# Running the first MLP pair in seven products inside the output projection's last units, and dealing out the query norms and gate logarithms

## The chip, the core and the metric

The kernel runs on one core of one Trainium2 chip. The metric is the device time of one execution in microseconds (us). Before the change the median of three runs is 2124.6 us (2124.42 to 2124.96).

Engines are named as in the profile: PE is TensorE's matmul, PEld its weight load, DVE is VectorE, ACT is ScalarE, POOL is GpSimd, and SP is the engine whose queue issues nearly all DMAs here.

## The reference: two layers of a hybrid encoder

256 rows of 2048 numbers go through two layers. All of it is float32:

```python
for l in range(N_A):                       # layer A
    u = rms_norm(h, a_norm_g[l])
    proj = u @ a_w_in[l]
    q, k, v, fz = jnp.split(proj, [D, 2 * D, 3 * D], axis=-1)
    q = rms_norm(q.reshape(B, S, H, Dh), a_q_g[l])
    k = rms_norm(k.reshape(B, S, H, Dh), a_k_g[l])
    logf = jax.nn.log_sigmoid(fz + a_b_f[l])
    o = forgetting_attention(q, k, v, logf)
    h = h + o.reshape(B, S, D) @ a_w_out[l]
    h = h + sq_relu_mlp(h, mlp_norm_g[layer], mlp_w1[layer], mlp_w2[layer])
kv = rms_norm(h, kv_norm_g) @ kv_w          # shared keys and values
...
for l in range(N_B):                       # layer B: own queries, chunked attention
    u = rms_norm(h, b_norm_g[l])
    q = rms_norm((u @ b_w_q[l]).reshape(B, S, H, Dh), b_q_g[l])
    o = chunked_relbias_attention(q, k_sh, v_sh, b_rel[l])
    h = h + o.reshape(B, S, D) @ b_w_out[l]
    h = h + sq_relu_mlp(h, mlp_norm_g[layer], mlp_w1[layer], mlp_w2[layer])
```

`sq_relu_mlp` is `relu(rms_norm(h) @ w1)**2 @ w2` with 8192 hidden columns. The two MLPs are most of the matmul work.

## The kernel before

**Units and panels.** All weights come in *units*: 128 partitions by 1024 numbers, 512 KB, which are two 128-row slices of the contraction by 512 output columns. A float32 unit is split in two parts that TensorE multiplies fast: `hi` (ACT, line 183) and `lo = raw - hi` (DVE, line 184). The activations are split the same way, and each product is three matmuls, hi·hi, hi·lo and lo·hi (`three`, lines 388 to 390). A *panel* is 512 output columns for all 256 rows: eight units, each with 12 matmuls of 128x512 (2 slices, 2 row blocks, 3 matmuls). A panel accumulates in a pair of PSUM banks.

**Order.** The kernel writes the order of PE, DVE, ACT and SP by hand, and each engine runs its list in that order. One iteration of the program handles one unit: `fetch` issues `hi` and `lo` of the unit two places ahead and keeps three raw loads under way, then come the matmuls of this unit, and then `run_fill` runs one entry of the list `fill`. In `fill` stand the small jobs of norms, attention, residuals and transposes, so one entry runs in each unit. There are three `hi` and `lo` buffers: a `hi` waits until PE is done with the unit three places before. When a panel is complete, its two banks are evacuated (`evac`).

**Seven products.** In the MLPs two panels form a *pair* (halves `a` and `b`). The first two units of each half (four units, a 2x2 block scheme in rows and columns) can be computed with seven products in place of eight, by sums of weights and of activations. Each of the seven is a *form* of 6 matmuls. Their weights are 11, T3, T2, T1, 21, T4 and 22, run in this order as f0 to f6. The four raw blocks 11, 12, 21 and 22 are loaded by `bring` (line 739), some 9 to 6 plain units before f0. The sums T1 = 12 − 11, T3 = 22 − 12, T2 = T3 + 11 and T4 = 21 − T2 are made by `make` on DVE (line 754). The forms T3, T2, T1 and 22 multiply by sums of activations: `S` for the layer's normalized input, `Sh` for hidden values (`sums`, line 229: four DVE sums, two ACT copies as the hi part, and one unit later two DVE subtractions as the lo part, line 246). Forms f0 to f3 are woven between the last units (b5, b6, b7) of the pair before; f4 to f6 between the pair's own units. In the kernel before, the first pair of each MLP is not `fast`: it runs all 16 units plainly (a0 a1 b0 b1 …) and leaves only b6 and b7 for weaving. An MLP has 16 pairs: four chunks of hidden columns, in each two pairs of w1 and two of w2.

**The way into the MLP.** The output projection (`stage`, line 424) has four panels: 0 and 1 woven unit by unit, then 2, then 3. After each, `next_x` (line 301) adds the residual, sums squares, transposes the 512 columns (`blocks32` on DVE, then `carry`: `rows` writes to DRAM, `columns` reads back in four DMAs), and two units run `split_turned` (line 249): ACT scales into `bias` (line 254), ACT rounds to hi (line 257), DVE makes lo (line 258). Panel 0 also makes `S`. Panel n gives the activations of contraction units 2n and 2n + 1. `st1.inverse` makes the row scale that the second half of the MLP needs.

**Queries of layer B.** `head_norm` (line 430) squares a panel (ACT), sums per head (DVE, line 444), takes the power on POOL (line 449), multiplies and transposes (DVE, lines 453 and 277). For query panel 0 it first copies the PSUM banks (`qc`, line 437), because panel 2 takes the same banks at once.

**Gate logarithms.** `gates` (line 603) hands `logs` to `fill` in three steps: sums of the products (lines 628 to 634), then Exp, Ln and the scan (636 to 639), then the write to DRAM (642 to 645).

**Buffers that matter.** Pool `qkv` holds two each of tags `k` and `v` (attention; the raw blocks of a pair), `bias` (attention, `split_turned`, T1 and T3). Pool `prob` has one room `p`: attention's, then `Sh`. PSUM has pairs `acc0`, `acc1`, the two banks `s` of attention's logits, and `po`. A pair takes `acc0` and alternately `acc1` or `s`.

Of the kernel before, what the change touches and what calls it, by code (L numbers as in the profile page):

```python
# [15 lines left out]
P = 128  # L16
# [30 lines left out]
def trunk(ctx: ExitStack, tc: tile.TileContext, xT, xr, gs, hg, bf, wgate, w_in, w_oa, w1a, w2a,  # L47
# [53 lines left out]
    def queue(src, first, woven):  # L101
        u = [src[i] for i in range(first, first + KT // UA * NG)]
        n = KT // UA
        if woven:
            u[: 2 * n] = [u[i + q * n] for i in range(n) for q in range(2)]
        units.extend(u)
# [5 lines left out]

    class Pair:

        def __init__(self, src, first, fast, late, third):
            self.src = [[src[first + q * 8 + u] for u in range(8)] for q in range(2)]
            self.fast, self.late, self.third, self.ps, self.t = fast, late, third, None, {}

        def own(self):
            if not self.fast:  # L120
                head, rest = "a0 a1 b0 b1 a2 a3 b2 b3 a4 a5 b4 b5 a6 a7", "b6 b7"
            elif self.late:
                head, rest = "a2 f4 a3 f5 b2 f6 b3 a4 a5 b4 a6 a7", "b5 b6 b7"
            else:
                head, rest = "a2 f4 a3 f5 a4 f6 a5 a6 a7 b2 b3 b4", "b5 b6 b7"
            return [[(self, "abf".index(i[0]), int(i[1])) for i in t.split()] for t in (head, rest)]

    def plan_mlp(w1, w2):
        n, pairs = w1.shape[0] // NCH, []
        for c in range(NCH):  # L130
            for src, late in ((w1, False), (w2, True)):
                for q in range(2):
                    pairs.append(Pair(src, c * n + 16 * q, bool(pairs), late and q == 0, len(pairs) % 2 == 1))
        plan, rest = [], []
        for p in pairs:
            head, mine = p.own()
            if p.fast:
                f = [(p, 2, i) for i in range(4)]
                if len(rest) == 3:
                    plan += [f[0], rest[0], f[1], rest[1], f[2], rest[2], f[3]]  # L140
                else:
                    plan += [f[0], f[1], rest[0], f[2], rest[1], f[3]]
            plan += head
            rest = mine
# [6 lines left out]
    queue(w_oa, 0, True)  # L151
    plan_a = plan_mlp(w1a, w2a)
    queue(w_qb, 0, True)
    for i in range(w_kv.shape[0]):
        units.append(w_kv[i])
    queue(w_ob, 0, True)
    plan_b = plan_mlp(w1b, w2b)
# [143 lines left out]
    def next_x(n, r2, stats, which, into, kept=None, fs=None):  # L301
        add_h = residual(n, r2)
        zt = []
        fs = fs if n == 0 else None

        def use(flipped=False, which=which, into=into):
            t = zt[1].rearrange("p (i k b c) -> p k b i c", i=4, k=GH, b=NB)
            if flipped:
                t = t[:, :, :, ::-1, ::-1]
            return split_turned(t, n, which, into, fs)  # L310

        def turn():
            zt.extend(turned("s" if kept is not None and n >= 2 else "q"))
            for b in range(NB):
                blocks32(h[b][:, n * 512 : (n + 1) * 512], zt[0], b)

        def f(b, ps):
            add_h(b, ps)
            if b == NB - 1:
                step = steps(use)  # L320
                add_fill([[lambda b=b: stats.add(b, n) for b in range(NB)], [turn],
                          [lambda: add_fill(carry(*zt) + [[]] * (3 if n == 1 else 1) + [[step]] * 2 + ([] if fs is None else [[], [], [step], [step]]))]])
                if kept is not None:
                    kept.append(use)
        return f
# [85 lines left out]
    def panels(x, evacs, before=None):  # L411
        ps = [acc_pair() for _ in evacs]
        for u in range(KT // UA):
# [10 lines left out]
    def stage(x, evacs, woven):  # L424
        if woven:
            panels(x, evacs[:2])
        for e in evacs[2 if woven else 0 :]:
            panels(x, [e])

    def head_norm(stats, z, dst, late=0, copied=False, gap=0):  # L430
        rest = []

        def f(b, ps):
            src = ps
            if copied:
                src = wk.tile([P, 512], F32, name="qc", tag="wk")
                V.tensor_copy(src, ps)
            sq = wk.tile([P, 512], F32, name="sq", tag="wk")
            S.activation(sq, src, AF.Square)
            ss = sm.tile([P, GH], F32, name="ss")  # L440
            rn = sm.tile([P, GH], F32, name="rn")

            def total():
                V.tensor_reduce(ss, sq.rearrange("p (a d) -> p a d", a=GH), axis=AX.X, op=ALU.add)

            def norm():
                vv = sm.tile([P, GH], F32, name="vv")
                V.tensor_scalar(vv, ss, 1.0 / P, stats().e[:, b : b + 1], op0=ALU.mult, op1=ALU.add)  # L448
                G.tensor_tensor(rn, vv, mhalf, op=ALU.pow)  # L449

            def turn():
                qn = wk.tile([P, 512], F32, name="qn", tag="wk")
                V.tensor_tensor(qn.rearrange("p (a d) -> p a d", a=GH), src.rearrange("p (a d) -> p a d", a=GH),
                                rn.unsqueeze(2).to_broadcast([P, GH, P]), op=ALU.mult)
                blocks32(qn, z, b)

            rest.append((total, norm, turn))
            if b == NB - 1:
                for total, norm, _ in rest:
                    total()  # L460
                    if not late:
                        norm()
                add_fill([[]] * (late - 1) + ([[n for _, n, _ in rest]] if late else []) + [[]] * gap + [[t] for _, _, t in rest] + carry(z, dst))
        return f
# [138 lines left out]
    def gates(x, st):  # L603
# [21 lines left out]
        def logs():  # L625
# [11 lines left out]
            S.activation(z, z, AF.Ln, bias=1.0)  # L637
            V.scalar_tensor_tensor(z, u, 0.0, z, op0=ALU.min, op1=ALU.subtract)
# [9 lines left out]
        def turn_c():  # L648
            pc = ps_o.tile([P, 512], F32, name="pt", tag="po")
            ct["cq"] = const.tile([P, NB, H], F32, name="cq")  # L650
            for b in range(NB):
# [5 lines left out]
                [], [step], [step], [step], [], [turn_c]]  # L657
# [33 lines left out]

    def mlp(plan, x, Sx, st, last):
        hids = [[] for _ in range(NCH)]
# [33 lines left out]
        pairs = list(dict.fromkeys(p for p, _, _ in plan))  # L727

        def open_pair(p):
# [3 lines left out]
            p.ps = [acc_pair(0), acc_pair(2 if p.third else 1)]  # L733
# [5 lines left out]
        def bring(p, name):  # L739
            t = qkv.tile([P, UN], F32, name="w" + name, tag="kv"[name[1] == "2"], bufs=2)  # L740
            SY.dma_start(t, p.src[int(name[1]) - 1][int(name[0]) - 1])
            p.t[name] = t

        def make(p, name):
            t = p.t
            if name in ("T1", "T3"):
                t[name] = qkv.tile([P, GH * REL], F32, name="w" + name, tag="bias", bufs=2)[:, :UN]
            elif name == "T2":
                t[name] = t["12"]
            else:  # L750
                t[name] = t["11"]
            a, b, op = {"T1": ("12", "11", ALU.subtract), "T3": ("22", "12", ALU.subtract),
                        "T2": ("T3", "11", ALU.add), "T4": ("21", "T2", ALU.subtract)}[name]
            V.tensor_tensor(t[name], t[a], t[b], op=op)  # L754

        ahead = {9: (bring, "12"), 8: (bring, "11"), 7: (bring, "22"), 6: (bring, "21"), 5: (make, "T1"), 2: (make, "T3")}
        starts = [i for i, it in enumerate(plan) if it[1:] == (2, 0)]
        for i, (p, q, u) in enumerate(plan):
# [9 lines left out]
            else:  # L768
# [8 lines left out]
                if nxt is not None:  # L777
                    d = sum(1 for it in plan[i:nxt] if it[1] < 2)
                    if d in ahead:
                        do, name = ahead[d]  # L780
                        do(plan[nxt][0], name)
# [10 lines left out]
    stage(o, [next_x(n, None, st1, 1, x1, fs=S1) for n in range(NG)], True)  # L792
    add_fill([[], [], [], [st1.inverse]])
# [10 lines left out]
    for g in range(NG):  # L804
        box = {}

        def f(b, ps, box=box, g=g):
            if b == 0:
                z, lq = turned("z")
                box["lq"], box["f"] = lq, head_norm(lambda: st2, z, lq, copied=g == 0, gap=2 * (g == 1))  # L810
            box["f"](b, ps)
            if b == NB - 1:
                add_fill([[]] * (7 + 2 * (g == 1)) + [[lambda: qs.append(scale_q(box["lq"], 1, g))]])
        evs.append(f)
    stage(xb, evs, True)
# [23 lines left out]
    stage(o, [next_x(n, None, st3, 4, x3, fs=S3) for n in range(NG)], True)  # L839
    add_fill([[], [], [], [st3.inverse]])  # L840
# [66 lines left out]
```

## Time and profile before

| | |
|---|---|
| median of three runs | 2124.6 us |
| the profiled execution, its own time | 2125.99 us |
| its span | 2124.2 us |
| granted TensorE clock | 1.00 |
| DVE busy | 1574.4 us (74%) |
| ACT busy | 1185.6 us (56%) |
| moved by DMA | 491.61 MB, mean 231 GB/s |

How to read the rows below. A group's row has the line, engine, operation, names written and read, count, then busy us, mean ns of one, and idle time before it with the releaser. A row of the timeline has the start and length in us, the engine, line and names, and in brackets the idle time before it and what ended it. A row of a stretch has its bounds and length, then busy time and count of PE, PEld, DVE, ACT and POOL, the clock, the DMA share and GB/s. Starts are counted from the start of the span.

The order of the work in time: layer A's projections and attention to about 340 us, its output projection to 387, MLP A to about 1108, queries, keys, values and attention of layer B to about 1390, its output projection to 1439, MLP B to the end.

### The profile page before, as it was taken

Reading aid. Unit: us, or ns where it says so; the run is one execution under the profiler, and the core shown is the slowest. Engines: PE = TensorE matmul, PEld = TensorE weight load, DVE = VectorE, ACT = ScalarE, POOL = GpSimd, SP = SyncE. Lnnn points to the kernel's source line nnn. Section 1 sums busy time; section 2 is a strip of 40 time slices with the busy share of each in tenths; the row PEclk is TensorE's granted clock in tenths of the full one; section 3 lists DMA queues with packets and bytes.
Section 4 is the critical chain, followed back from the end, with each engine's and each line's share of the span. In section 5 each row is a group of like instructions: output and inputs, shape, how many; then the busy total and the mean of one; then the engine's idle time right before and its main releaser. Section 6 shows DMA issues by size and latency. Waiting matters only on the chain.

```text
span 2124.2 us, 25852 instructions
## 1 busy us (share of the span) xinstructions
PE 2109.3 (99%) x9338; PEld 1740.9 (82%) x9338; DVE 1574.4 (74%) x1795; ACT 1185.6 (56%) x1421; POOL 48.2 (2%) x47
## 2 busy tenths in 40 slices
PE   9999999999999999999999999999999999999999
PEld 7788888878888888888888888887788888888887
DVE  6677666688787777778767577766877887877775
ACT  6544455565466465556575444455654654664663
POOL 1011000000000000000001000000000000000000
PEclk9999999999999999999999999999999999999999
DMA  8787777876676577577678777777766666766764
GB/s 281 230 256 230 239 246 237 268 229 225 203 247 225 201 246 240 186 236 269 190 227 268 236 234 234 233 244 246 248 224 211 239 225 207 249 220 200 247 239 147
DMA packets 183889, 491.61 MB, mean 231 GB/s; under 512 B 36929, under 2 KB 73937, under 8 KB 183761
## 3 DMA queue, kind: packets, MB, share of 16 engines
q1 hardware_dynamic: 183760, 489.96, 70.7%
q8 instruction: 73, 1.20, 0.2%
q14 instruction: 56, 0.45, 0.1%
HBM read 450.01 MB, written 39.87 MB: 231 GB/s over the span
## 4 chain that ended last, share of the span: by engine, by line
PE 93%; DVE 3%; DMA 1%; ACT 1%; issue 1%; SPq 0%; ACTq 0%; DVEq 0%
PE acc L390 25%; PE acc L389 25%; PE acc L388 25%; PE s L389 6%; PE s L390 6%; PE s L388 6%; DVE lo L184 1%; DMA raw<-in_w_in 1%; ACT hi L183 1%; PE po L532 1%; PE s L501 1%; PE po L533 0%; PE s L500 0%; DVE wT L754 0%; DVE z L277 0%
## 5 line engine op out<-in xcount | busy, mean ns | idle before, releaser
L184 DVE TENSOR_TENSOR lo<-raw,hi 128x1024 fp32r<-128x1024 f32 (+1 forms) x650 | 789.8, 1217 | 328.9 <-ACT hi L183 308.5
L183 ACT ACTIVATE hi<-raw 128x1024 fp32r<-128x1024 f32 (+1 forms) x650 | 685.7, 1057 | 524.7 <-PE acc L390 423.5
L388 PE MATMUL acc<-hi,act 128*128 128x512 f32 x2356 | 926.2, 393 | 0.1
L389 PE MATMUL acc<-lo,act 128*128 128x512 f32 x2356 | 918.7, 390 | 4.9 <-DVE lo L184 4.8
L390 PE MATMUL acc<-hi,act 128*128 128x512 f32 x2356 | 917.3, 389 | 0.4 <-DVE act L226 0.4
L389 PEld LDWEIGHTS acc<-lo,act 128*128 128x128 f32 x2356 | 442.4, 188 | 102.1 <-DVE lo L184 10.9
L390 PEld LDWEIGHTS acc<-hi,act 128*128 128x128 f32 x2356 | 442.2, 188 | 92.8 <-DVE act L226 0.8
L388 PEld LDWEIGHTS acc<-hi,act 128*128 128x128 f32 x2356 | 442.5, 188 | 91.6 <-ACT hi L183 1.1
L183 ACT ACTIVATE hi<-w 128x1024 fp32r<-128x1024 f32 x150 | 159.2, 1061 | 203.2 <-PE acc L390 107.4
L184 DVE TENSOR_TENSOR lo<-w,hi 128x1024 fp32r<-128x1024 f32 x150 | 183.2, 1222 | 107.2 <-ACT hi L183 107.2
L389 PE MATMUL s<-lo,act 128*128 128x512 f32 x416 | 162.1, 390 | 3.2 <-DVE lo L184 3.2
L390 PE MATMUL s<-hi,act 128*128 128x512 f32 x416 | 161.9, 389 | 0.0
L388 PE MATMUL s<-hi,act 128*128 128x512 f32 x416 | 161.8, 389 | 0.0
L183 ACT ACTIVATE hi<-wT 128x1024 fp32r<-128x1024 f32 x60 | 63.7, 1062 | 72.9 <-PE acc L390 34.0
L184 DVE TENSOR_TENSOR lo<-wT,hi 128x1024 fp32r<-128x1024 f32 x60 | 73.5, 1225 | 40.0 <-ACT hi L183 39.7
L389 PEld LDWEIGHTS s<-lo,act 128*128 128x128 f32 x416 | 78.1, 188 | 20.2 <-DVE lo L184 4.0
L388 PEld LDWEIGHTS s<-hi,act 128*128 128x128 f32 x416 | 78.1, 188 | 16.2
L390 PEld LDWEIGHTS s<-hi,act 128*128 128x128 f32 x416 | 78.1, 188 | 16.1
L754 DVE TENSOR_TENSOR wT<-w,w 128x1024 f32<-128x1024 f32 x60 | 73.1, 1219 | 0.0
L449 POOL TENSOR_TENSOR rn<-vv,mhalf 128x4 f32<-128x4 f32 x32 | 42.8, 1352 | 393.0 <-DVE vv L448 393.0
L535 ACT ACTIVATE act<-po 128x256 fp32r<-128x256 f32 x32 | 12.3, 385 | 70.2 <-PE po L533 70.2
L536 DVE TENSOR_TENSOR act<-po,act 128x256 fp32r<-128x256 f32 x32 | 13.6, 424 | 34.4 <-ACT act L535 34.4
(161 smaller groups left out, 1362.7 us busy)
## 6 DMA issues: line engine op xcount, KB each, us to landing
raw<-in_w1a SPq DMA_DIRECT2D x100, 512.0 KB, 4.7
raw<-in_w1b SPq DMA_DIRECT2D x100, 512.0 KB, 4.6
raw<-in_w2a SPq DMA_DIRECT2D x96, 512.0 KB, 4.4
raw<-in_w2b SPq DMA_DIRECT2D x96, 512.0 KB, 4.3
raw<-in_w_in SPq DMA_DIRECT2D x94, 512.0 KB, 4.5
raw<-in_w_kv SPq DMA_DIRECT2D x64, 512.0 KB, 4.3
turn<-z SPq DMA_DIRECT2D x60, 512.0 KB, 4.5
q<-turn SPq DMA_DIRECT2D x168, 128.0 KB, 4.1
```

Of the source, the lines that this page charges most:

```text
L183: S.activation(hi[:, c], raw[:, c], AF.Copy)
L184: V.tensor_tensor(lo[:, c], raw[:, c], hi[:, c].bitcast(F32), op=ALU.subtract)
L388: TE.matmul(ps, xh, wh, start=first, stop=False, **kw)
L389: TE.matmul(ps, xh, wl, start=False, stop=False, **kw)
L390: TE.matmul(ps, xl, wh, start=False, stop=last, **kw)
L449: G.tensor_tensor(rn, vv, mhalf, op=ALU.pow)
L501: TE.matmul(s[:, P : 3 * P], q[:, a, P:T], k[:, a], start=True, stop=True)
L532: TE.matmul(po[:, :T], v[:, 0, a * P : (a + 1) * P], pT[:, :2], start=True, stop=False)
L535: S.activation(o[i][:, 0], po[:, :T], AF.Copy)
L536: V.tensor_tensor(o[i][:, 1], po[:, :T], o[i][:, 0].bitcast(F32), op=ALU.subtract)
L754: V.tensor_tensor(t[name], t[a], t[b], op=op)
```

## The change

1. The first pair of each MLP is `fast` too. The last three units (5, 6, 7) of the output projection's panel 3 leave `stage` and become a `Tail`, whose units are woven between the forms f0 to f3 of that pair. The pair's own order is the new one called "early".
2. `prepare` is called in every unit of the output projection, so that the pair's four raw blocks are loaded 9 to 6 plain units before f0 and its T1 and T3 are made 5 and 2 before. T1 and T3 of this pair lie in the room `p`. The second pair's T1 is made 4 units before.
3. For panel 3 of the output projection, `next_x` puts the squares and the transposes in one unit, `rows` in the next, `columns` in the one after that, then the row scale, an empty entry and the two split steps.
4. The pairs take `acc` and alternately `s` the other way round (`third`), beginning with `base`, the bank pair that is next in turn. Query panel 0 of layer B takes this pair, panel 1 the banks `s`; the copies `qc` are gone.
5. `head_norm` has `apart`: for query panels 0 and 1, square, sum and norm of each row block get a unit of their own, 0 and 2 units after the panel, then the turns. `scale_q` moves by two units for both.
6. `logs` has a fourth step: Exp and Ln are one step and the scan the next. The first step runs one unit earlier.

```diff
+    class Tail:
+        fast = None
+        def __init__(self, src, first):
+            self.src = [[src[first + u] for u in range(KT // UA)]]
...
+            self.head = {"early": "a2 f4 a3 f5 b2 f6 b3 a4 b4 a5 a6 a7", "late": "a2 f4 a3 f5 b2 f6 b3 a4 a5 b4 a6 a7",
+                         "": "a2 f4 a3 f5 a4 f6 a5 a6 a7 b2 b3 b4"}[order]
...
-    def plan_mlp(w1, w2):
+    def plan_mlp(w1, w2, tail):
...
+        pairs[1].t1 = 4
+        plan, rest = [], [(tail, 0, u) for u in range(KT // UA - 3, KT // UA)]
         for p in pairs:
+            f = p.items("f0 f1 f2 f3")
+            plan += [f[0], rest[0], f[1], rest[1], f[2], rest[2], f[3]] + p.items(p.head)
+            rest = p.items("b5 b6 b7")
...
+                if then is not None:
...
+                    add_fill([[lambda b=b: stats.add(b, n) for b in range(NB)] + [turn], [rows], [lambda: way[1]()],
+                              [then], [], [step], [step]])
+                    return
...
+                turns = [[t] for _, _, _, t in rest] + carry(z, dst)
+                if apart is not None:
+                    add_fill([[]] * apart + [[s, t, n] for s, t, n, _ in rest] + turns)
+                    return
...
             S.activation(z, z, AF.Ln, bias=1.0)
+            yield
             V.scalar_tensor_tensor(z, u, 0.0, z, op0=ALU.min, op1=ALU.subtract)
...
-                [], [step], [step], [step], [], [turn_c]]
+                [step], [step], [step], [step], [], [turn_c]]
...
+    def prepare(p, d, first=True):
+        if first and d == 9:
+            p.room = prob.tile([P, 9 * 3 * P], F32, name="wTT", tag="p", bufs=1)
+        step = {9: (bring, "12"), 8: (bring, "11"), 7: (bring, "22"), 6: (bring, "21"), p.t1: (make, "T1"), 2: (make, "T3")}.get(d)
+        if step:
+            step[0](p, step[1])
...
-    stage(o, [next_x(n, None, st1, 1, x1, fs=S1) for n in range(NG)], True)
-    add_fill([[], [], [], [st1.inverse]])
+    stage(o, [next_x(n, None, st1, 1, x1, fs=S1, then=st1.inverse if n == NG - 1 else None) for n in range(NG)], tail=tail_a, plan=plan_a)
...
-                box["lq"], box["f"] = lq, head_norm(lambda: st2, z, lq, copied=g == 0, gap=2 * (g == 1))
+                box["lq"], box["f"] = lq, head_norm(lambda: st2, z, lq, apart=(0, 2, None, None)[g])
...
+    turns[0] = 1 - turns[0]
+    stage(xb, evs, (1 - turns[0], 2))
```

In the written orders of the two kernels, PE has 9160 rows in place of 9172. DVE has, from the last unit of panel 3 that is no tail on, the order: sums of S, the panel's split, `lo` of T3, the sum T2, `lo` of tail unit 6, the two lo parts of S. SP issues the four raw blocks of the first pair between the last five raw units of panels 2 and 3, and the same loads as before in all.

More of the change, by code (lines that the diff above doesn't have):

```diff
@@ L99, in trunk, with queue @@
     units = deque()
-    def queue(src, first, woven):
-        u = [src[i] for i in range(first, first + KT // UA * NG)]
+    def queue(src, m):
+        u = [src[i] for i in range(m)]
         n = KT // UA
-        if woven:
-            u[: 2 * n] = [u[i + q * n] for i in range(n) for q in range(2)]
+        u[: 2 * n] = [u[i + q * n] for i in range(n) for q in range(2)]
         units.extend(u)
@@ L111, in __init__ @@
             self.pair, self.name = pair, ("11", "T3", "T2", "T1", "21", "T4", "22")[i]
+    class Tail:
+        fast = None
+        def __init__(self, src, first):
+            self.src = [[src[first + u] for u in range(KT // UA)]]
     class Pair:
-        def __init__(self, src, first, fast, late, third):
+        fast = True
+        def __init__(self, src, first, order, third):
             self.src = [[src[first + q * 8 + u] for u in range(8)] for q in range(2)]
-            self.fast, self.late, self.third, self.ps, self.t = fast, late, third, None, {}
@@ L119, in own @@
[L119 to L126, printed above, removed]
-    def plan_mlp(w1, w2):
+            self.third, self.ps, self.t, self.room, self.t1 = third, None, {}, None, 5
@@ L132, in plan_mlp @@
                 for q in range(2):
-                    pairs.append(Pair(src, c * n + 16 * q, bool(pairs), late and q == 0, len(pairs) % 2 == 1))
-        plan, rest = [], []
+                    pairs.append(Pair(src, c * n + 16 * q, (late if pairs else "early") if q == 0 else "", len(pairs) % 2 == 0))
+        pairs[1].t1 = 4
+        plan, rest = [], [(tail, 0, u) for u in range(KT // UA - 3, KT // UA)]
         for p in pairs:
[L136 to L144, printed above, removed]
+            f = p.items("f0 f1 f2 f3")
+            plan += [f[0], rest[0], f[1], rest[1], f[2], rest[2], f[3]] + p.items(p.head)
+            rest = p.items("b5 b6 b7")
@@ L299, in turned, with next_x @@
         return z, qkv.tile([P, GH * T], F32, name=name, tag=name, bufs=2)
-    def next_x(n, r2, stats, which, into, kept=None, fs=None):
+    def next_x(n, r2, stats, which, into, kept=None, fs=None, then=None):
         add_h = residual(n, r2)
@@ L409, in form_products, with panels @@
             three(ps[i not in (4, 5)][i in (1, 5)], xh, xl, hi, lo, g, i < 2 and g == 0, i < 2 and g == 1, skip_group_check=True)
-    def panels(x, evacs, before=None):
-        ps = [acc_pair() for _ in evacs]
-        for u in range(KT // UA):
+    def panels(x, evacs, before=None, after=None, which=(None, None), tail=None):
+        ps = [acc_pair(i) for i in which[: len(evacs)]]
+        for u in range(KT // UA - (3 if tail else 0)):
             if before:
@@ L462, in f @@
                         norm()
-                add_fill([[]] * (late - 1) + ([[n for _, n, _ in rest]] if late else []) + [[]] * gap + [[t] for _, _, t in rest] + carry(z, dst))
+                add_fill([[]] * (late - 1) + ([[n for _, _, n, _ in rest]] if late else []) + turns)
         return f
@@ L725, in turn_hidden @@
             return f
-        pairs = list(dict.fromkeys(p for p, _, _ in plan))
+        pairs = [p for p, q, u in plan if (q, u) == (2, 0)]
         def open_pair(p):
@@ L838, in trunk @@
     st3, x3, S3 = RowStats("n"), [], []
-    stage(o, [next_x(n, None, st3, 4, x3, fs=S3) for n in range(NG)], True)
-    add_fill([[], [], [], [st3.inverse]])
+    stage(o, [next_x(n, None, st3, 4, x3, fs=S3, then=st3.inverse if n == NG - 1 else None) for n in range(NG)], tail=tail_b, plan=plan_b)
     def store(n, r2):
```

99 lines of the change are left out of this document (57 added, 42 removed).

## The prediction

> **What bounds the kernel now.** I read the page first, then busy time by stretches, then the waits of the stretches that lose time, then single rows around them.
>
> ```profile
> span 2124.2 us, 25852 instructions
> PE 2109.3 (99%) x9338; PEld 1740.9 (82%) x9338; DVE 1574.4 (74%) x1795; ACT 1185.6 (56%) x1421; POOL 48.2 (2%) x47
> L389 PE MATMUL acc<-lo,act 128*128 128x512 f32 x2356 | 918.7, 390 | 4.9 <-DVE lo L184 4.8
> L754 DVE TENSOR_TENSOR wT<-w,w 128x1024 f32<-128x1024 f32 x60 | 73.1, 1219 | 0.0
> ```
>
> TensorE sets the end. Its 390 ns per matmul is not its price, because matmuls overlap; the price comes from the stretches (time, then PE's busy time and count, then PEld, DVE, ACT):
>
> ```profile
> 420.00:475.00 55.00, 53.20 (x230) 42.49 (x229) 44.32 (x46) 33.74 (x36) 0.00 (x0) 1.00 0.69 225
> 475.00:1100.00 625.00, 625.00 (x2759) 517.13 (x2758) 484.51 (x469) 369.02 (x398) 0.69 (x1) 1.00 0.69 226
> 1100.00:1125.00 25.00, 23.70 (x103) 18.97 (x103) 20.70 (x28) 14.07 (x18) 5.40 (x4) 1.00 0.57 188
> 1472.00:1530.00 58.00, 55.71 (x241) 44.26 (x240) 46.48 (x48) 35.82 (x39) 0.00 (x0) 1.00 0.69 223
> ```
>
> In 475 to 1100 us nothing waits: 625 / 2759 = 0.2265 us per matmul at clock 1.00. So a plain unit (12 matmuls) takes 2.72 us and a form (6) 1.36 us. Against this, 420 to 475 loses 55 − 230 × 0.2265 = 2.9 us, 1100 to 1125 1.7 us, 1472 to 1530 3.4 us. These are the first pair that runs in seven products (twice, one in each MLP) and the query panels. The waits of 415 to 475 and of 1425 to 1530, first row each (us, times, longest):
>
> ```profile
> PE s L389 <- DVE lo L184: 1.6, 2, 1.4
> ...
> PE s L389 <- DVE lo L184: 2.1, 2, 1.8
> ```
>
> The longest ones lie where `Sh` is made (470 and 1523 us); with the restart behind them they are 1.6 and 2.0 us. The rest, 1.3 and 1.4 us, lies at the pair's start. PE waits each time for `lo`, which queues in VectorE's written order. VectorE's order therefore decides the price of every part below.
>
> **Part 1, the products.** Per MLP four units (48 matmuls) become seven forms (42). Twelve matmuls fewer: 12 × 0.2265 = **−2.7 us**. The added work is per MLP three `lo`, three `hi` and four L754 sums, about 1.14 us apiece on VectorE; it counts only where it delays a `lo`. [...]
>
> **Part 2, the later start.** The old first seven-product pair had only two units (b6 b7) between its forms and now has three, in the pattern of the stall-free stretch. I drop its waits: 1.3 + 1.4 = **−2.7 us**.
>
> **Part 3, query norms.** The first query panel loses its two copies, and squares, sums and norms of both woven panels go out over four units.
>
> ```profile
> 1108.68 1.23 DVE L258 TENSOR_TENSOR act<-bias,act 128x1024 fp32r<-128x1024 f32 x1 [0.67 <-ACT act L257]
> 1109.83 1.28 DVE L437 COPY qc<-acc 128x512 f32<-128x512 f32 x2
> 1111.21 0.69 DVE L444 TENSOR_REDUCE ss<-sq 128x4 f32<-128x512 f32 x1
> ```
>
> Per unit VectorE then has at most a `lo` (1.14), a qn and transpose (0.72 + 0.63) and a sum and norm (0.86), 3.4 us, beside units of 2.0 to 2.5, under PE's 2.72 on the mean. The whole loss goes: **−1.7 us**. The panels that follow take other PSUM banks, so they do not wait for the later turn.
>
> **Part 4, gate logarithms.** The first step moves a unit earlier; Exp and Ln get a step of their own.
>
> ```profile
> 60.86 0.38 ACT L630 ACTIVATE gz<-s 16x256 f32<-16x256 f32 x1 [1.92 <-DVE gu L629]
> 61.27 0.41 DVE L631 TENSOR_TENSOR gu<-gu,gz 16x256 f32<-16x256 f32 x1 [0.44 <-ACT gz L630]
> 63.42 1.28 ACT L637 ACT_TABLE_LOAD   x1
> ```
>
> VectorE is busy from 52 to 70 us but for this 0.44 us, and the ScalarE work (the table load too) already ran beside it. The same VectorE work in another order ends no sooner; its earlier half now stands ahead of a `lo`. **0**, bounds −0.9 and +0.5.
>
> **Part 5, the sums S: the decisive one.** The forms T3, T2, T1 and 22 read S, made from the first normalized panel. S stays where it was (its sums in the last unit before the tail, its `lo` halves a unit later), but its first reader moves from long after to right behind. VectorE, then PE, around it now:
>
> ```profile
> 382.77 1.23 DVE L258 TENSOR_TENSOR act<-bias,act 128x1024 fp32r<-128x1024 f32 x1 [2.59 <-ACT act L257]
> 383.92 1.22 DVE L184 TENSOR_TENSOR lo<-raw,hi 128x1024 fp32r<-128x1024 f32 x1
> 385.05 1.28 DVE L246 TENSOR_TENSOR S<-sum,S 128x512 fp32r<-128x512 f32 x2
> ```
> ```profile
> 384.36 0.39 PE L388 MATMUL acc<-hi,act 128*128 128x512 f32 x1
> 385.19 0.50 PE L389 MATMUL acc<-lo,act 128*128 128x512 f32 x1 [0.45 <-DVE lo L184]
> 385.52 0.39 PE L390 MATMUL acc<-hi,act 128*128 128x512 f32 x1
> ```
>
> Already now PE waits here: 0.83 + 0.33 us between starts instead of 2 × 0.2265, so 0.7 us. In the changed order the `lo` of 383.92 is T3's. Behind it stand the sum T2 and the next unit's `lo`, and then S. From 383.92 to 385.05 one such step takes 1.13 us, so S is complete at 385.05 + 1.28 + 2 × 1.13 = 388.6. PE is there earlier: three plain units start from 376.20 (384.36 − 3 × 2.72) on, and in the change these are a plain unit, form 11 and a tail unit, so T3 starts at 376.20 + 2.72 + 1.36 + 2.72 = 383.0. Its third matmul, due at 383.45, reads S. The wait is 5.15 us and 0.1 for the restart, in place of 0.7: +4.5 per MLP, **+9.0 us**. Bounds: 1.3 per MLP if only T3's `lo` (385.14) held it, 5.0 if more comes between. After so long a wait the next three forms find their operands ready.
>
> **Part 6, four loads moved ahead.** The weights of the first pair's forms (4 × 512 KB) are issued some 20 us earlier, past two carries and in front of the last raw units on SP's queue. The DMA's row of 354 to 372 us (tenths busy in 40 slices), and its sum; then the sum and the raw row of 402 to 416 us, where the next pair's four loads run today:
>
> ```profile
> DMA  9999997999999999999999999999999979895200
> ...
> DMA packets 2251, 5.03 MB, mean 279 GB/s; under 512 B 258, under 2 KB 1282, under 8 KB 2250
> ```
> ```profile
> DMA packets 1700, 4.63 MB, mean 331 GB/s; under 512 B 186, under 2 KB 698, under 8 KB 1699
> ...
> raw<-in_w1a SPq DMA_DIRECT2D x5, 512.0 KB, 7.3
> ```
> ```profile
> 368.75 1.06 ACT L183 ACTIVATE hi<-raw 128x1024 fp32r<-128x1024 f32 x1 [0.15 <-DMA raw<-in_w_oa]
> ```
> ```profile
> 377.49 1.23 DVE L184 TENSOR_TENSOR lo<-raw,hi 128x1024 fp32r<-128x1024 f32 x1 [1.07 <-ACT hi L183]
> ```
>
> The DMA is full until 370, and at 368.75 a `hi` already waits for its raw unit. Two of the four loads come ahead of that unit: 1.05 MB at 331 GB/s is 3.2 us, at 410 2.6. VectorE's slack before the sums is 1.07 us, and the sum T3 (1.13) fills it, so S can come up to 2.7 us later. Against it, the next pair's loads share the DMA with one carry, raws take 7.3 us, and no wait shows there. Between 0 and 2.7 I take the middle, 1.3 per MLP: **+2.6 us**. [...]
>
> **Part 7, the last normalized panel.** It is finished two units closer to its reader: its second split step now runs in the unit just before a6. Such a step in today's record:
>
> ```profile
> 393.50 1.06 ACT L183 ACTIVATE hi<-raw 128x1024 fp32r<-128x1024 f32 x1 [0.86 <-ACT bias L254]
> 394.47 0.89 ACT L254 ACTIVATE bias<-q,gsb 128x256 f32<-128x256 f32 x2
> 395.39 1.06 ACT L257 ACTIVATE act<-bias 128x1024 fp32r<-128x1024 f32 x1
> ...
> 396.49 1.23 DVE L258 TENSOR_TENSOR act<-bias,act 128x1024 fp32r<-128x1024 f32 x1 [0.67 <-ACT act L257]
> ```
>
> From the `hi`, which starts some 0.25 us into the unit, to the end at 397.72 are 4.2 us. a6's third matmul is due 2.72 + 0.45 = 3.2 us into it and gets its operand at 4.45: 1.3 per MLP, **+2.6 us** (0 to 3.2). The columns of this panel wait on SP one step sooner for the rows; raws stand behind, with a lead of three loads, and cost nothing.
>
> **Part 8, Sh.** The first pair's `a` half ends later, so Sh's sums now stand in one unit with two transposes, and one more split stands before it.
>
> ```profile
> 462.99 1.31 ACT L243 ACTIVATE Sh<-sum 128x512 fp32r<-128x512 f32 x2 [2.96 <-DVE sum L238]
> ```
>
> ScalarE waits there for VectorE and VectorE then for ScalarE. By 1.14 per `lo`, split or sum, 1.5 for S's sums, 1.2 for Sh and 1.24 for transposes, VectorE has 10.8 us in the three units before form 11 (8.16 us of PE). I keep the 1.6 and 2.0 us as they are and add **+0.4**; bounds −3.6 and +2.
>
> **Sum.** −2.7 − 2.7 − 1.7 + 0 + 9.0 + 2.6 + 2.6 + 0.4 = +7.5. The profiled execution took 2125.99 us, 1.8 outside its span, and lies 1.4 above the median; the change applies to both, so the median goes from 2124.6 to **2132.1 us**.
>
> **The rivals.**
> - *More of it:* the loads cost their full 2.7 per MLP and Sh another 1.5 in all: +7.5 + 2.8 + 1.5, **2136**. The full DMA row speaks for it, the waitless pair of 402 to 416 against.
> - *A wash:* S's wait comes as worked out, but raws are in time (−2.6) and Sh's waits go, since its sums start sooner (−4.0): +0.9, **2125.5**.
> - *Faster, S held by T3's `lo` alone:* S's wait is 1.3 per MLP over today's, since its halves land before 385.2; raws in time, Sh's waits gone: −7.1 + 2.6 + 2.6 − 3.6 = −5.5, **2119**. It decides from S complete 3 us sooner than the rows give. S follows a `lo` that itself ends at 385.14, which speaks against it.
>
> **How the numbers follow.** Forecast 0.42, more 0.24, wash 0.20, faster 0.14. The range 2121.5 to 2137.5 leaves out most of the fast case and the tail of the slow one. Differences under 0.2% (4.2 us) count as none: the fast case lies below 2120.4; the wash and a tenth of the forecast (0.04) lie within; the rest, 0.62, lies above. The forecast's own bounds are 2127 to 2137.
>
> **What would show it.** Right: the third matmul of the first `s<-hi,S` group waits some 5 us for L248 in both MLPs, and a6 a good 1 us for an L260; no waits at 430 and 1482 or in the query panels; PE has 9326 instructions. Wrong: T3's group starts without a wait, or its wait is for `lo`; the `hi` before it never waits for `raw`; PE waits in the steady stretch after the first two pairs.

## The result and the profile after

The changed kernel is slower: median 2141.89 us (2141.41 to 2142.22, 4 runs) against 2124.51 us for the kernel before (2122.54 to 2124.96, 4 runs). The ratio is 1.0083, 95% interval 1.0066 to 1.0101. The forecast was 2132.1 us with a range up to 2137.5: the sign is right, and the loss is 17.4 us where 7.5 was forecast. The profiled execution took 2141.82 us.

The page of the changed kernel, first its span, then busy time and count of each engine:

```profile
span 2140.0 us, 25845 instructions
PE 2112.8 (99%) x9326; PEld 1742.0 (81%) x9326; DVE 1591.9 (74%) x1811; ACT 1194.1 (56%) x1431; POOL 48.7 (2%) x47
```

PE has the 9326 instructions that were forecast, and its busy share is 99% as before: on this page 16 us of loss cannot be seen. They are seen in the stretches (bounds, length, busy time and count of PE, PEld, DVE, ACT, POOL, clock, DMA share, GB/s):

```profile
372.00:396.00 24.00, 16.92 (x61) 12.21 (x60) 17.32 (x21) 14.66 (x20) 0.00 (x0) 0.86 0.58 211
420.00:440.00 20.00, 19.16 (x84) 15.23 (x83) 14.89 (x15) 11.88 (x15) 0.00 (x0) 1.00 0.57 201
485.00:1110.00 625.00, 625.00 (x2759) 517.21 (x2759) 484.43 (x469) 368.85 (x397) 0.70 (x1) 1.00 0.68 226
1110.00:1135.00 25.00, 25.00 (x112) 20.71 (x111) 19.81 (x25) 14.68 (x20) 5.89 (x4) 1.00 0.68 220
1431.00:1459.00 28.00, 20.67 (x74) 15.23 (x73) 19.12 (x23) 15.71 (x21) 0.00 (x0) 0.88 0.52 173
```

Most of it lies in two places. At 0.2265 us each, 61 matmuls need 13.8 of the 24 us from 372 on, and 74 need 16.8 of the 28 us from 1431 on. These are the tail units and first forms of the two MLPs. The clock there is 0.86 and 0.88, in a kernel that otherwise ran at 1.00. The steady stretch still has 2759 matmuls in 625 us, and the query panels at 1110 have become free of loss.

To put it in one table I took for each PE row by how much it starts later than 0.227 us after the row before it, left out what is under 0.03 us, and added up the rest by stretches of each trace. The table has these sums, the time lost, in us:

| stretch, us | what is there | before | after |
|---|---|---|---|
| 0–100 | first products, gate logarithms | 6.94 | 7.13 |
| 350–400 | panel 3, S, first forms of MLP A | 0.71 | 10.37 |
| 415–440 | first pair of MLP A; in the changed kernel its a6 | 1.49 | 1.40 |
| 460–490 | Sh of MLP A | 1.62 | 1.98 |
| 1090–1140 | query panels | 1.84 | 0 |
| 1400–1470 | panel 3, S, first forms of MLP B | 0.71 | 11.66 |
| 1470–1500 | first pair of MLP B; in the changed kernel its a6 | 1.51 | 1.40 |
| 1500–1545 | Sh of MLP B | 2.27 | 2.02 |
| sum | | 17.1 | 36.0 |

The loss grows by 18.9; twelve matmuls fewer save 2.7; 16.2 is left, and the spans differ by 15.9.

What PE waits for from 372 to 396 us, in the view of waits (total us, times, longest):

```profile
PE s L402 <- DVE S L248: 2.7, 1, 2.7
PE acc L401 <- DVE lo L186: 2.0, 2, 1.2
PE s L400 <- ACT hi L185: 1.5, 1, 1.5
PE s L401 <- DVE lo L186: 1.0, 1, 1.0
```

The wait for S at T3's third matmul is the one that was forecast, and the waits of three more rows stand ahead of it. The timeline of PE there, in which I follow the starts:

```profile
387.24 0.49 PE L400 MATMUL s<-hi,S 128*128 128x512 f32 x1 [1.47 <-ACT hi L185]
388.69 0.79 PE L401 MATMUL s<-lo,S 128*128 128x512 f32 x1 [0.95 <-DVE lo L186]
392.17 0.79 PE L402 MATMUL s<-hi,S 128*128 128x512 f32 x1 [2.68 <-DVE S L248]
392.76 0.63 PE L400 MATMUL s<-hi,S 128*128 128x512 f32 x1
393.18 0.63 PE L401 MATMUL s<-lo,S 128*128 128x512 f32 x1
393.61 0.63 PE L402 MATMUL s<-hi,S 128*128 128x512 f32 x1
```

The last three rows wait for nothing, and yet start 0.42 to 0.43 us apart instead of 0.2265. That is the half clock: from 388.60 to 395.43 us the granted clock is 0.50. VectorE in the same place, and then the two `hi` on ScalarE that waited for raw units:

```profile
387.42 1.22 DVE L186 TENSOR_TENSOR lo<-wTT,hi 128x1024 fp32r<-128x1024 f32 x1
388.56 1.22 DVE L737 TENSOR_TENSOR w<-wTT,w 128x1024 f32<-128x1024 f32 x1
389.69 1.22 DVE L186 TENSOR_TENSOR lo<-raw,hi 128x1024 fp32r<-128x1024 f32 x1
390.83 1.28 DVE L248 TENSOR_TENSOR S<-sum,S 128x512 fp32r<-128x512 f32 x2
```
```profile
367.35 1.06 ACT L185 ACTIVATE hi<-raw 128x1024 fp32r<-128x1024 f32 x1 [3.58 <-DMA raw<-in_w_oa]
372.29 1.06 ACT L185 ACTIVATE hi<-raw 128x1024 fp32r<-128x1024 f32 x1 [1.86 <-DMA raw<-in_w_oa]
```

The order on VectorE is the one that was worked out: T3's `lo`, the sum T2, the tail unit's `lo`, S, a step of 1.14 us each and no idle time between. Only the start is off: T3's `lo` starts at 387.42, not 383.92, and S is complete at 390.83 + 1.28 = 392.1, not 388.6. The `hi` that starts at 372.29 is the one that started at 368.75 before. So everything here is 3.5 us late, and it comes late from the DMA, as experiment 1 shows.

### The profile page after: what moved, and what is told of

Read it like the earlier page. It is cut to its first block, busy times and chain, and to the rows that moved or that the text cites. A ratio compares the mean times of both kernels' runs of the same rounds, so it can differ in the third digit from the quotient of the medians.

```text
span 2140.0 us, 25845 instructions
## 1 busy us (share of the span) xinstructions
PE 2112.8 (99%) x9326; PEld 1742.0 (81%) x9326; DVE 1591.9 (74%) x1811; ACT 1194.1 (56%) x1431; POOL 48.7 (2%) x47
## 4 chain that ended last, share of the span: by engine, by line
PE 92%; DMA 3%; DVE 3%; ACT 1%; SPq 1%; issue 1%; ACTq 0%; DVEq 0%
PE acc L402 24%; PE acc L401 24%; PE acc L400 24%; PE s L402 6%; PE s L400 6%; PE s L401 6%; DVE lo L186 1%; DMA raw<-in_w_in 1%; DMA q<-turn 1%; PE po L558 1%; PE s L527 1%; ACT hi L185 0%; DMA raw<-in_w_oa 0%; DMA raw<-in_w_ob 0%; PE po L559 0%
## 5 line engine op out<-in xcount | busy, mean ns | idle before, releaser
L186 DVE TENSOR_TENSOR lo<-raw,hi 128x1024 fp32r<-128x1024 f32 (+1 forms) x642 | 780.5, 1217 | 324.1 <-ACT hi L185 300.9
L400 PE MATMUL acc<-hi,act 128*128 128x512 f32 x2304 | 907.4, 394 | 1.8 <-ACT hi L185 0.7
L401 PE MATMUL acc<-lo,act 128*128 128x512 f32 x2304 | 899.2, 390 | 7.1 <-DVE lo L186 6.9
L402 PE MATMUL acc<-hi,act 128*128 128x512 f32 x2304 | 898.4, 390 | 1.6 <-DVE act L260 1.0
L401 PEld LDWEIGHTS acc<-lo,act 128*128 128x128 f32 x2304 | 433.5, 188 | 102.1 <-DVE lo L186 12.7
L400 PEld LDWEIGHTS acc<-hi,act 128*128 128x128 f32 x2304 | 433.6, 188 | 93.1 <-ACT hi L185 2.0
L402 PEld LDWEIGHTS acc<-hi,act 128*128 128x128 f32 x2304 | 433.1, 188 | 93.1 <-DVE act L260 1.9
L185 ACT ACTIVATE hi<-w 128x1024 fp32r<-128x1024 f32 x160 | 169.7, 1060 | 202.3 <-PE acc L402 108.8
L186 DVE TENSOR_TENSOR lo<-w,hi 128x1024 fp32r<-128x1024 f32 x160 | 195.4, 1221 | 105.9 <-ACT hi L185 105.9
L401 PE MATMUL s<-lo,act 128*128 128x512 f32 x448 | 174.5, 389 | 0.9 <-DVE lo L186 0.9
L400 PE MATMUL s<-hi,act 128*128 128x512 f32 x448 | 174.4, 389 | 0.0
L402 PE MATMUL s<-hi,act 128*128 128x512 f32 x448 | 174.3, 389 | 0.0
L186 DVE TENSOR_TENSOR lo<-wT,hi 128x1024 fp32r<-128x1024 f32 x60 | 73.5, 1226 | 39.3 <-ACT hi L185 39.1
L401 PEld LDWEIGHTS s<-lo,act 128*128 128x128 f32 x448 | 84.1, 188 | 19.1 <-DVE lo L186 1.7
L400 PEld LDWEIGHTS s<-hi,act 128*128 128x128 f32 x448 | 84.1, 188 | 17.4
L402 PEld LDWEIGHTS s<-hi,act 128*128 128x128 f32 x448 | 84.1, 188 | 17.4
L737 DVE TENSOR_TENSOR wT<-w,w 128x1024 f32<-128x1024 f32 x60 | 73.1, 1218 | 0.0
L469 POOL TENSOR_TENSOR rn<-vv,mhalf 128x4 f32<-128x4 f32 x32 | 43.3, 1366 | 388.7 <-DVE vv L468 388.6
L737 DVE TENSOR_TENSOR w<-w,w 128x1024 f32<-128x1024 f32 x32 | 39.0, 1217 | 0.0
```

The source lines that it names most:

```text
L185: S.activation(hi[:, c], raw[:, c], AF.Copy)
L186: V.tensor_tensor(lo[:, c], raw[:, c], hi[:, c].bitcast(F32), op=ALU.subtract)
L400: TE.matmul(ps, xh, wh, start=first, stop=False, **kw)
L401: TE.matmul(ps, xh, wl, start=False, stop=False, **kw)
L402: TE.matmul(ps, xl, wh, start=False, stop=last, **kw)
```

## The experiments

Each experiment edits the changed kernel; its main lines are shown, and "..." marks what is left out. The ratios compare with the kernel before, run beside it.

**1. The sums of S two units earlier, the four loads six units earlier, and both.** These take the two suspected causes apart.

```diff
-... ([] if fs is None else [[], [], [step], [step]])
+... ([] if fs is None else [[step], [step]])
```

> Theory: the changed kernel loses most where form T3's third matmul waits for the lo half of S (L248): 1.6 + 1.2 + 3.2 us of waits in one place in each MLP, and then runs 3 to 6 us at about half clock. Here the four sums and the split of S run two units earlier, nothing else changes. Then the wait for L248 is gone in both MLPs, and what is left at T3 is at most the late raw unit (about 1 to 2 us); the spacing of 0.43 us behind it is gone too. Worth 2 x (5 to 6) + 4.5 = 13 to 17 us: 2125 to 2129 us. Rival: the four loads in front of the raw units decide (DMA); then S early changes little, since PE waits for hi of late units instead: 2138 us or more.

```diff
+        e = 6 if first else 0
-        step = {9: (bring, "12"), 8: (bring, "11"), 7: (bring, "22"), 6: (bring, "21"), ...
+        step = {9 + e: (bring, "12"), 8 + e: (bring, "11"), 7 + e: (bring, "22"), 6 + e: (bring, "21"), ...
```

> The four raw blocks of the first pair are loaded six units earlier than in the changed kernel, ahead of the two carries; all else stays. Theory: the late raw units cost some 3 us per MLP (waits of 1.3 and 1.6 us between starts at 374 and 378 us, and S late by 3.5 us). Then hi no longer waits for raw_oa at 367 and 372 us, S is complete near 388.6 instead of 392.1 us, the wait for L248 stays at about 5 us in all, and the kernel takes 2133 to 2136 us. If the loads cost nothing it stays at 2141; if they are the whole of it, it falls below 2128.

The third kernel has both edits:

> S two units earlier and the four loads six units earlier. Theory: both waits are gone, what is left of the change is 12 matmuls less (-2.7), the waits at the next pair gone (-2.7), the query panels (-1.7), a6's wait (+2.8) and 0.7 us of the old wait at S gone in each MLP: 2118 to 2121 us, faster than before. Rival: a further wait takes their place at the same units (VectorE too full): 2124 or more.

Measured: 2134.59 us with S early (ratio 1.0043, 1.0028 to 1.0058), 2133.45 us with the loads early (1.0039, 1.0024 to 1.0054), 2127.57 us with both (1.0014, 1.0005 to 1.0024). The loss of 350–400 and 1400–1470 falls from 10.37 and 11.66 to 5.25 and 6.39, to 6.97 and 8.30, and to 2.91 and 3.47 (0.6 of the 3.47 is a6's wait, which begins at 1469 us there). With the loads early, the time is in the expected range. With S early it lies between theory and rival, and with both the rival holds: a further wait took the place.

With the loads early, the waits of PE from 370 to 395 us, S on VectorE, and the `hi` that was late:

```profile
PE s L402 <- DVE S L248: 2.8, 1, 2.8
PE s L401 <- DVE lo L186: 1.0, 1, 1.0
PE s L400 <- ACT hi L185: 0.6, 1, 0.6
```
```profile
385.43 1.28 DVE L248 TENSOR_TENSOR S<-sum,S 128x512 fp32r<-128x512 f32 x2
```
```profile
366.62 1.04 ACT L185 ACTIVATE hi<-raw 128x1024 fp32r<-128x1024 f32 x1
```

The `hi` waits for no DMA, and the waits for what is made of late raw units (the `acc` row) are gone: 3.4 us less in each MLP. The wait for S stays, since its order on VectorE stays: 0.74 + 1.23 + 3.24 us over the regular spacing at T3's three matmuls, 5.2 us, and 5.7 in MLP B. With S early:

```profile
PE acc L401 <- DVE lo L186: 2.7, 2, 1.8
PE s L401 <- DVE lo L186: 0.8, 1, 0.8
PE s L400 <- ACT hi L185: 0.2, 1, 0.2
```

No row waits for S. The longest wait, 1.8 us, isn't the loads' either: it is for a tail unit's `lo` (from 383.17 us), which now stands behind S and the sum T3 (from 382.03). So each edit alone leaves the other cause, and with both this third one is left:

```profile
PE acc L401 <- DVE lo L186: 2.0, 2, 1.8
```
```profile
378.04 1.29 DVE L248 TENSOR_TENSOR S<-sum,S 128x512 fp32r<-128x512 f32 x2
379.24 1.22 DVE L737 TENSOR_TENSOR wTT<-w,w 128x1024 f32<-128x1024 f32 x1
380.38 1.22 DVE L186 TENSOR_TENSOR lo<-raw,hi 128x1024 fp32r<-128x1024 f32 x1
```

The sum T3 (L737) stands between S and the `lo` of a tail unit, and PE waits 1.8 us for that `lo`. The stall that was taken away at one matmul came back, smaller, at the next operand that queues behind the same work.

**2. The last panel's splits one unit earlier as well.** This edit adds to the two above that the empty entry behind the row scale is left out, so that a6 has its operand a unit sooner.

```diff
-                              [then], [], [step], [step]])
+                              [then], [step], [step]])
```

> As the one with both, and the last panel's two split steps run one unit earlier (the empty entry before them is dropped). Theory: a6's third matmul no longer waits for L260 (1.4 us in each MLP): 2.8 us under the one with both, 2115 to 2118 us. Rival: its columns have not landed by then, the split waits for the DMA and the wait stays as it was.

Measured: 2124.23 us, ratio 0.9995 (0.9986 to 1.0005). In the changed kernel the view of waits has from 420 to 440 us

```profile
PE acc L402 <- DVE act L260: 0.5, 1, 0.5
PE acc L400 <- ACT act L259: 0.3, 1, 0.3
```

and over the regular spacing 1.40 us are lost there, in each MLP. With this edit both rows are gone and the loss is 0: the expected mechanism, though not the expected time, since the kernel with both edits was slower than expected already. The three repairs together give back what the change cost and no more.

**3. The same wait, but TensorE kept busy in it.** This tells the half clock from the wait. The kernel adds products that nobody reads ahead of T3's group, first 20, then 8, once per MLP; they go to a PSUM tile of their own.

```diff
+                if u == 1 and p is pairs[0]:
+                    spare = ps_o.tile([P, 512], F32, name="pt", tag="po")
+                    for _ in range(20):
+                        TE.matmul(spare, p.x[0][:, 0, :P], p.x[0], start=True, stop=True)
                 form_products(p.ps, hi, lo, p.x, p.fs, u)
```

> The changed kernel with 20 matmuls more (128x512, on operands that are ready, into a bank that nobody reads) put on PE between the last matmul of the tail unit and form T3, in both MLPs: 4.5 us of work in the stretch in which PE waits for S. Nothing else changes, so S is complete at the same time. Theory: the matmul spacing of 0.43 us after the wait (8 times in the first MLP, 15 in the second) comes from PE having idled; kept busy, it goes on at 0.227 us, and the clock of the stretches after the wait reads 1.00 in place of 0.57 and 0.54. About 1.6 + 3.1 us less: 2137 us beside 2141.9. Rival: it is the DMA or the late operands that stretch the matmuls; then the 0.43 stays and the time too.

Measured: 2135.55 us, ratio 1.0054 (1.0039 to 1.007). That is 6.3 us under the changed kernel's first median and 4.6 under its second (2140.13, experiment 6), although it does 40 matmuls more. Its stretches around S (MLP A, the time right behind it, MLP B):

```profile
384.00:391.50 7.50, 6.10 (x27) 4.75 (x26) 6.45 (x7) 4.46 (x5) 0.00 (x0) 1.00 0.39 86
391.50:396.00 4.50, 4.50 (x21) 3.72 (x20) 2.88 (x3) 2.61 (x3) 0.00 (x0) 1.00 0.31 101
1448.00:1455.00 7.00, 7.00 (x32) 5.72 (x32) 5.34 (x6) 3.67 (x4) 0.00 (x0) 1.00 0.39 140
```

The clock is 1.00 all through, and behind S stand 21 matmuls in 4.50 us. The changed kernel has behind the same wait 10 in 4 us, and in MLP B 16 in 6.5:

```profile
392.00:396.00 4.00, 3.83 (x10) 3.08 (x11) 1.83 (x3) 1.54 (x2) 0.00 (x0) 0.57 0.34 127
1451.00:1457.50 6.50, 6.46 (x16) 5.12 (x17) 3.48 (x3) 1.54 (x2) 0.00 (x0) 0.54 0.31 102
```

The extra spacing over 0.2265 us of the matmuls that wait for nothing adds up to 1.65 us in A and 2.9 in B. That is some 4.5 us which no row of the view of waits shows.

With 8 products in place of 20:

> As the one with 20 filling matmuls, but with 8 (1.8 us), so that PE still waits in one piece for some 3 to 4 us before the third matmul of T3. Theory, if the clock falls after a few us without matmuls: the clock stays at 1.00 or falls in one MLP only, and the time lies between 2137 and 2141 us. Rival, any idling of 3 us is enough: both dips stay, 2141.

Measured: 2139.12 us, ratio 1.0071 (1.0056 to 1.0086). Eight products fill the time in which `hi` was late. What is left in each MLP is 0.9 us of waiting for `lo`, one matmul, and 3.0 us of waiting for S, as long as in the changed kernel's B. The clock still falls in both MLPs, to 0.66 from 391 to 396 us and to 0.56 from 1448 to 1454, as the rival had it: what was filled was not enough.

**4. The query norms put back, the logarithms put back.** These are single runs, and each is read by its own stretch alone; experiment 6 shows why.

```diff
-... head_norm(lambda: st2, z, lq, apart=(0, 2, None, None)[g])
+... head_norm(lambda: st2, z, lq, late=(0, 3, 0, 0)[g], copied=g == 0)
```

> The changed kernel with the query norms of panels 0 and 1 made in one go again, panel 0's copies too. Theory: the waits for lo in the query panels come back, 1.3 to 1.9 us in all, where the changed kernel has none. Rival: they had gone because of the other banks, and stay away: under 0.4 us.

Panel 0's copies `qc` come back with it, and `scale_q` moves back by two units; the PSUM banks stay as changed. Between 1110 and 1140 us the restored norms have this wait, where the changed kernel has none:

```profile
PE acc L401 <- DVE lo L186: 0.6, 1, 0.6
```

The loss of 1090–1140 is 1.40 us again, against 0 in the changed kernel and 1.84 before. So the dealing out, with the copies gone, is worth 1.4 us; 1.7 was forecast. The time was 2144.75 us.

```diff
-            yield
...
-                [step], [step], [step], [step], [], [turn_c]]
+                [], [step], [step], [step], [], [turn_c]]
```

> The changed kernel with the gate logarithms in three steps again. Theory: VectorE's work between 52 and 70 us is the same in either order, so the two waits for lo there keep their sum of about 0.95 us (over 0.2265 us spacing, restarts with them) within 0.4 us. Rival: the fourth step saves most of it, then it is 1.5 us or more with three steps.

The loss of 50–80 us is 1.26 us with the logarithms put back, 1.26 in the changed kernel and 1.24 before: no effect to be seen. The time was 2136.6 us.

**5. T1 and T3 of the first pair earlier too.** On top of the three repairs, these two sums are made 10 and 9 units before f0, so that no sum of weights stands between S and the tail's `lo`; the third pair's T1 is made one unit sooner.

```diff
+        pairs[2].t1 = 6
...
-        if first and d == 9:
+        if first and d == 11:
...
+        t1, t3 = (10, 9) if first else (p.t1, 2)
```

> The three repairs (S two units earlier, loads six units earlier, the last panel's split one unit earlier), and T1 and T3 of the first pair made 10 and 9 units ahead in units where VectorE has only a lo, and T1 of the third pair one unit earlier. Theory: the wait that took S's place (2.2 us between starts in the last unit before T3, with 0.5 and 0.5 us beside it) comes from T3's sum standing between S and the next lo; it falls by about 1.1 us or more in each MLP, and the waits at Sh (2.0 us) by about 1. 3 to 6 us under the kernel with three repairs: 2118 to 2121 us, faster than before. Rival: ScalarE's part of S holds the next hi and the wait stays: 2123 to 2125.

Measured: 2119.21 us (11 runs), ratio 0.9974 (0.9965 to 0.9983), the fastest kernel of this study and faster than both. PE's waits from 370 to 395 us and the stretch (this kernel's lines stand one lower, so its L187 and L402 are L186 and L401 of the others):

```profile
PE acc L402 <- DVE lo L187: 1.0, 2, 0.7
PE s L402 <- DVE lo L187: 0.3, 1, 0.3
```
```profile
365.00:395.00 30.00, 28.74 (x124) 22.82 (x123) 25.03 (x28) 21.44 (x33) 0.00 (x0) 1.00 0.58 185
```

2.09 and 1.94 us are lost at the two places, where the changed kernel loses 10.37 and 11.66. At Sh it is 1.22 and 1.23, where the kernel with three repairs loses 2.01 and 1.99. The change itself (seven products, dealt-out norms) was sound; the place of what feeds it was not.

**6. The changed kernel once more.**

> The changed kernel as it is, on the chip and in the rounds of the one with 8 filling matmuls. Theory: 2140 to 2143 us; about 10 us of lost spacing between 350 and 400 us, and a clock under 1.00 after the wait for S in both MLPs, whose length need not be the same from one execution to the next. Rival: single executions scatter by several us at the same place, because the late raw units do.

Measured: 2140.13 us (2138.79 to 2141.21), ratio 1.0074 (1.0057 to 1.009). The same code lost 9.44 and 11.73 us at the two places, against 10.37 and 11.66, and in the kernels with norms or logarithms put back, whose code there is the changed kernel's, 12.21 and 9.80, 9.77 and 10.07. How late a raw unit lands, and how long the clock stays down (the mean clock of its eight executions is 0.996 or 0.997), differ by a few us between executions. The first 100 us alone lose from 4.99 to 9.23 us in the twelve traces. So single times of two such kernels are not compared here.

## Why the prediction was right in its sign and too low

**Right by their own steps.** Part 1 (products): 9326 matmuls, and the steady stretch at the same 0.2265 us. Part 2 (pair start): the loss of 1.49 and 1.51 us there belongs to the pair's start before the change and to a6 after it; no wait is left at the start. Part 3 (query norms): 1.84 to 0, of which 1.40 came back with the norms. Part 4 (logarithms): 0, and putting them back changed nothing. Part 5 (S): with the loads out of the way T3's three matmuls lose 5.2 and 5.7 us where the order before lost 0.7, so 9.5 in all against 9.0, and S stands on VectorE behind the three steps that were named. The wait is not one but three, for `hi`, `lo` and S; it is one chain, so the sum holds. Part 7 (a6): 1.40 per MLP against 1.3, in two waits in place of one. Part 8 (Sh): +0.36 and −0.25 against +0.4 in all; no experiment moved Sh's sums, so this agrees by its number alone. The rival in which S waits for T3's `lo` alone is refuted by the four VectorE rows.

**The step that failed: Part 6, the loads.** The prediction bounded the delay of a raw unit by the DMA rate of another stretch (402 to 416 us in the kernel before: 331 GB/s in the mean, 410 in several slices of its second half, so 2.6 to 3.2 us), cut that to 2.7, and took the middle between that and 0 because a pair at 402 to 416 showed no wait. The measured cost is 3.4 us per MLP (10.37 to 6.97 and 11.66 to 8.30 with the loads early), so +6.8 in the sum in place of +2.6. The right row stood in the prediction: the stretch of 354 to 372 us was full at 279 GB/s. At that rate the two loads that came ahead of the raw unit, 1.05 MB, take 3.8 us; it came 372.29 − 368.75 = 3.5 us later, which is 296 GB/s. Every rate that the prediction weighed, 331 to 410 GB/s, was too fast. The agreement is one of sizes: the unit was issued 2.0 us later (363.23 in place of 361.26 us) and took 1.6 us longer to land, and no run tells the queue's order from the DMA's rate. The DMA of 354 to 372 us in the changed kernel:

```profile
DMA packets 2290, 5.22 MB, mean 290 GB/s; under 512 B 251, under 2 KB 1275, under 8 KB 2289
...
raw<-in_w_oa SPq DMA_DIRECT2D x6, 512.0 KB, 8.8
w<-in_w1a SPq DMA_DIRECT2D x4, 512.0 KB, 8.2
q<-turn SPq DMA_DIRECT2D x8, 128.0 KB, 7.6
```

The four loads were added and the bytes moved grew by 0.19 MB only: the DMA was full, so what was put in front pushed the rest back. A raw unit now takes 8.8 us to land in the median, where it took 6.0; with the loads early it is 6.0 again. The pair of 402 to 416 us was the wrong cover to argue from: it shares the DMA with one carry, here there were two (the eight `q<-turn`). The forecast's choice of the middle was a choice against its own row.

**The step that was missing: the clock.** No part had a term for it, and the prediction's sum used 0.2265 us per matmul on both sides of the wait. The half clock cost some 4.5 us by the spacing, 4.6 to 6.3 by the times of experiment 3. With 4.5 for it and 4.2 more for the loads, 7.5 becomes 16.2. The medians differ by 17.4, the two profiled executions, by whose rows most of this is counted, by 15.8.

**The range.** The case "more of it" had the right mechanism for the loads, at 2.7 instead of 3.4; its end at 2136 was too low by this and the clock.

## What to carry to other kernels

Price a load that is moved ahead of others by its bytes at the rate that *that* stretch really moves; the stretch of 354 to 372 us had a full DMA at only 279 GB/s, and no slack. When a reader is moved next to its writer, count what stands between them on the writer's engine, then repair all links of the chain at once: load, sum and split each hid the next one here. Price the slow matmuls behind such a chain too: here TensorE was busy for 2.06 of the 7 us from 385 us on, and the matmuls behind started 0.43 us apart in place of 0.2265.

## What the runs showed of the hardware

I had not expected the clock to fall in waits this short. The changed kernel before the fall, at the low clock and after it, in MLP A and in MLP B:

```profile
384.40:388.60 4.20, 1.87 (x8) 0.98 (x6) 2.32 (x3) 4.17 (x6) 0.00 (x0) 1.00 0.60 169
388.60:395.43 6.83, 4.06 (x9) 2.88 (x10) 4.66 (x7) 2.18 (x4) 0.00 (x0) 0.50 0.21 77
395.43:400.00 4.57, 4.57 (x22) 3.76 (x21) 3.59 (x4) 2.48 (x3) 0.00 (x0) 1.00 0.34 115
1446.00:1450.20 4.20, 1.01 (x2) 0.37 (x2) 4.20 (x5) 2.55 (x4) 0.00 (x0) 1.00 0.04 9
1450.20:1457.03 6.83, 5.99 (x14) 4.74 (x15) 4.28 (x5) 1.54 (x2) 0.00 (x0) 0.50 0.30 88
1457.03:1460.00 2.97, 2.97 (x14) 2.45 (x14) 1.13 (x1) 1.93 (x2) 0.00 (x0) 1.00 0.37 152
```

In MLP A the clock is down from 388.60 on, and PE's wait for S begins at 389.48 (388.69 + 0.79) only: it had fallen already, at the end of the waits of 1.47 us for `hi` and 0.95 for `lo`. In MLP B it falls within the wait for S, which ends at 1451.04 after 2.97 us.

The length of a wait alone does not tell whether the clock falls. The kernel with three repairs has the same wait of 1.8 us for `lo` in both MLPs. Its stretch with the wait and the one behind it, in MLP A and in MLP B:

```profile
378.00:383.60 5.60, 3.42 (x15) 2.19 (x13) 4.77 (x6) 5.51 (x9) 0.00 (x0) 1.00 0.10 37
383.60:388.00 4.40, 4.37 (x18) 3.28 (x18) 4.40 (x4) 2.35 (x4) 0.00 (x0) 1.00 0.79 216
1428.00:1433.50 5.50, 3.59 (x16) 2.31 (x14) 4.79 (x6) 5.41 (x9) 0.00 (x0) 1.00 0.09 32
1433.50:1438.00 4.50, 4.50 (x13) 3.55 (x14) 4.45 (x4) 1.49 (x3) 0.00 (x0) 0.62 0.79 217
```

In MLP A the clock stays at 1.00, and 18 matmuls stand in 4.40 us behind the wait; in MLP B it is 0.62, with 13 in 4.50. The kernel with two repairs has this wait of 1.8 us in MLP B as well, with T3's sum before the `lo` there too, and its clock is 1.00 from 1424.86 to 1435.10. No run shows what decides between the two.

With two repairs, the four executions with a mean clock of 1.000 took 2124.19 to 2126.72 us (the profiled one, with the loss of 2.91 and 3.47, is one of them), and the six with 0.998 or 0.999 took 2127.07 to 2130.45: the same kernel had its clock down in one execution and not in the next. With three repairs all ten had 0.998 or 0.999, and their times don't part by it. This reading was made from the traces after the runs; the one experiment on it is the third, in which the clock stayed at 1.00 with 20 products in the wait and fell with 8.
